# Prompt attention of a hybrid decoder step: query blocks in pairs, value parts side by side as the stationary operand, a feature-major result

## The chip, the core and the metric

The kernel runs on one core of one Trainium2 chip. The metric is device time in microseconds (us) of one execution. Five engines with queues of their own take part: TensorE (PE, which multiplies and transposes), VectorE (DVE), ScalarE (ACT), GpSimd (POOL) and SyncE (SP, which here only issues transfers). Each engine takes the instructions of its queue in order, and an instruction that waits holds up all that stand behind it on its engine.

## What is computed

The program is one step of a two-layer decoder, for a prompt of 1024 tokens and for a sample group of 64 tokens. The part in question is the attention of layer 0 over the prompt: 8 heads, 96 query and key features (64 and 32 rotated ones), 64 value features, causal:

```python
s = (jnp.einsum('bqhd,bkhd->bhqk', qn, k_nope)
     + jnp.einsum('bqhr,bkr->bhqk', qr, k_rope)).astype(jnp.float32) * SOFTMAX_SCALE
s = jnp.where(mask[None, None], s, -jnp.inf)
p = jax.nn.softmax(s, axis=-1)
lat = jnp.einsum('bhqk,bkc->bqhc', p.astype(c.dtype), c)
return jnp.einsum('bqhc,chv->bqhv', lat, w_uv).reshape(b, tq, ATTN_OUT_DIM)
```

The kernel forms the values (latent rows times `w_uv`) first and multiplies the probabilities with them. The 512 attention features stand beside 512 features of a pooling mixer, and the 1024 together are the operand of one output projection.

## The kernel before

Everything is float32. Where two float32 operands meet on PE, a factor is split in two float32r parts (a cast, and a subtraction of the cast from the whole) whose products are added up; this is how scores and projections are done.

`prompt_attention` (from L696) goes through the heads one by one, and in a head through eight blocks i of 128 queries, in the order 7, 0, 6, 1, 5, 2, 4, 3, so that a long block alternates with a short one. Of each block:

- **Scores** (`scores`, L730 to L756): three matmuls of split parts for each chunk of keys, plus a bf16 matmul that lays the mask on the diagonal (L744), into a tile `s` of two PSUM banks, of which there are two. On DVE follow the row maximum `mx` (L750) and its product with the scale `nmx` (L751), on ACT the exponential `p` with the row sum (L753), on DVE the reciprocal `ri` of the sum (L754). P isn't normalised here.
- **Transposes** (`transposes`): PE turns each 128x128 block of P into the tile `ptp` (L764), up to four in one PSUM bank of which there are three (shared with the transposes of queries and keys, `qkt`), and one copy for each bank brings them to SBUF as `pT`: on ACT the banks that begin at key block 0 of i from 2 up (L769), on DVE the others (L767).
- **Values** (`values`, L777): for each key block one float32 matmul with `pT` as the stationary operand and 64 columns of `v_sb` moving. A float32 matmul is two passes on PE. The result has queries on the partitions, and DVE multiplies it by `ri` on its way out (L780).

The steps of different blocks overlap: block n's scores are written out ahead of block n-1's transposes and of block n-2's values, and between the blocks PE also makes the next head's transposed queries and keys (`prep`: transposes L720, a cast on ACT and a subtraction on DVE, L722 and L723). From this text a scheduler sets each engine's order. For each pair of heads SP stores the result token-major to `a_d` in DRAM (L804).

The sample group's attention comes next, and while it ends, the operands of the output projection are loaded (`mix_load`, L1120 on): the mixer's 512 features feature-major from `mix_d`, by chunk of tokens in two loads of two row groups each, cast on ACT and subtracted on DVE and POOL (L1127 to L1130), and the attention's token-major rows from `a_d` in loads of one or two token blocks, which PE transposes (`mix_tokens`, `atp`, L1147), four blocks for each 128 tokens, before the same split (L1150, L1151). All these loads go through three buffers `raw`.

Of the kernel before, what the change touches and what calls it, by code (L numbers as in the profile page):

```python
# [10 lines left out]
F32 = mybir.dt.float32  # L11
# [4 lines left out]
ALU = mybir.AluOpType  # L16
# [52 lines left out]
def bank(g, kind, name):  # L69
    """One PSUM bank of [128, 512], from the banks that serve this kind of use in turn."""  # L70
# [16 lines left out]
def wunit(g, ap, a, b, ring, lo=None):  # L87
    """One [128, a, b] block of a weight, split into two float32r parts that add up to it."""
# [41 lines left out]
def mm3(g, ps, pairs):  # L130
    """Accumulate float32 products of split operands: ((wh, wl), (xh, xl)) per row block."""
# [8 lines left out]
# ------------------------------------------------------------------ constants  # L140
# [19 lines left out]
def bcast_cols(g, ps, dg, r, out, n):  # L160
    """out[:, t * 128 + q] = r[q, t] on every partition: columns of per-token numbers as one row."""
# [7 lines left out]
# ------------------------------------------------------------------ feature-major norm  # L169
# The next product runs on x * gain; the row of 1 / rms, one number per token, multiplies its result.  # L170
# [37 lines left out]
def later(g, *fn):  # L208
    """Put off what the tensor engine would wait for."""
    g.late += fn  # L210
# [8 lines left out]
# ------------------------------------------------------------------ MLP  # L219
# [46 lines left out]
class OutProj:  # L266
    """y += w.T @ X per chunk, then the operands and the scale of the next product."""
# [46 lines left out]
def in_even(g, I, O, S, st_left):  # L314
# [3 lines left out]
    with ExitStack() as st:  # L318
# [90 lines left out]
        def zproc(ci, tb0, nb, zs, sq):  # L409
# [34 lines left out]
            # latent and rotary key  # L444
# [88 lines left out]
def pool_mixer(g, I, O, S, X, rs0, w, ps, ut, keep):  # L533
# [46 lines left out]
        # trailing window sums by doubling, the last group in two pieces  # L580
# [65 lines left out]
# ------------------------------------------------------------------ layer 0: keys and values  # L646
# [49 lines left out]
def prompt_attention(g, I, S, v_sb, first, mix0):  # L696
    nc = g.nc
    with ExitStack() as st:
# [8 lines left out]
        heads = {}  # L707
        ao = {}
# [911 lines left out]
```

## Time and profile before

| what | value |
|---|---|
| median of 3 runs | 2839.73 us (2837.73 to 2841.03) |
| span of the profiled execution | 2838.5 us |
| PE busy | 2713.7 us (96%) |
| DVE busy | 1807.2 us (64%) |
| ACT busy | 898.8 us (32%) |
| POOL busy | 396.8 us (14%) |
| prompt attention | about 234 to 421 us of the span |
| loads and splits for the output projection | about 785 to 822 us |

The span runs from the first to the last instruction of one profiled execution; the runs' median lies 1.2 us above it. Busy shares are over the whole span, most of which is the two MLPs and the recurrent layer; what the change touches are the two stretches in the last rows.

### The profile page before, as it was taken

Reading aid. Unit: us, or ns where it says so; the run is one execution under the profiler, and the core shown is the slowest. Engines: PE = TensorE matmul, PEld = TensorE weight load, DVE = VectorE, ACT = ScalarE, POOL = GpSimd, SP = SyncE. Lnnn points to the kernel's source line nnn. Section 1 sums busy time; section 2 is a strip of 40 time slices with the busy share of each in tenths; the row PEclk is TensorE's granted clock in tenths of the full one; section 3 lists DMA queues with packets and bytes.
Section 4 is the critical chain, followed back from the end, with each engine's and each line's share of the span. In section 5 each row is a group of like instructions: output and inputs, shape, how many; then the busy total and the mean of one; then the engine's idle time right before and its main releaser. Section 6 shows DMA issues by size and latency. Waiting matters only on the chain.

```text
span 2838.5 us, 43000 instructions
## 1 busy us (share of the span) xinstructions
PE 2713.7 (96%) x16801; PEld 2632.6 (93%) x16801; DVE 1807.2 (64%) x3501; ACT 898.8 (32%) x1878; POOL 396.8 (14%) x453
## 2 busy tenths in 40 slices
PE   7998999999999999999999998987999999999999
PEld 6887989888899999999999988887999999999998
DVE  7665657888755555555555579998365555555555
ACT  5334555666634111111111146655321111111111
POOL 4321001232212000000000044555200000000000
PEclk9999998999999999999999999998999999999999
DMA  5233102222251111111111121113111111111111
GB/s 161 62 108 108 38 16 76 62 61 59 70 136 42 45 45 46 42 49 39 49 40 48 36 90 35 35 31 109 47 47 50 39 48 39 49 38 51 38 38 64
DMA packets 200743, 162.07 MB, mean 57 GB/s; under 512 B 40331, under 2 KB 183148, under 8 KB 199763
## 3 DMA queue, kind: packets, MB, share of 16 engines
q1 hardware_dynamic: 200539, 159.31, 18.9%
q8 instruction: 133, 2.18, 0.3%
q14 instruction: 71, 0.58, 0.1%
HBM read 138.18 MB, written 21.21 MB: 56 GB/s over the span
## 4 chain that ended last, share of the span: by engine, by line
PE 62%; DVE 8%; ACT 1%; DMA 1%; POOL 1%; issue 1%; ACTq 0%; DVEq 0%; POOLq 0%
PE up L136 26%; PE dn L136 26%; PE op L136 6%; PE pgt L136 2%; DVE hs L1372 1%; DVE xl L182 1%; PE pg L136 1%; PE pu L136 1%; DVE v L1339 1%; DVE ta L1362 1%; DVE q L1392 0%; DVE y L250 0%; DVE vl L80 0%; ACT whA L79 0%; PE nbc L165 0%
## 5 line engine op out<-in xcount | busy, mean ns | idle before, releaser
L250 DVE TENSOR_TENSOR y<-y,dn 128x384 f32<-128x384 f32 (+1 forms) x768 | 404.9, 531 | 282.0 <-PE dn L136 279.7
L136 PE MATMUL dn<-hh,whB 128*128 128x384 f32 (+1 forms) x1536 | 505.8, 329 | 3.9 <-DVE y L250 3.8
L136 PE MATMUL up<-xh,wlA 128*128 128x384 f32 (+1 forms) x1536 | 501.6, 327 | 0.0
L136 PE MATMUL up<-xh,whA 128*128 128x384 f32 (+1 forms) x1536 | 501.1, 326 | 0.0
L136 PE MATMUL dn<-hh,wlB 128*128 128x384 f32 (+1 forms) x1536 | 501.0, 326 | 0.0
L136 PE MATMUL up<-xl,whA 128*128 128x384 f32 (+1 forms) x1536 | 501.0, 326 | 0.0
L136 PE MATMUL dn<-hl,whB 128*128 128x384 f32 (+1 forms) x1536 | 500.7, 326 | 0.0
L79 ACT CAST whB<-raw 128x1024 fp32r<-128x1024 f32 (+3 forms) x80 | 79.9, 1034 | 703.5 <-PE dn L136 663.4
L136 PEld LDWEIGHTS dn<-hh,whB 128*128 128x128 f32 x1536 | 288.3, 188 | 11.8 <-DVE y L250 11.6
L136 PEld LDWEIGHTS up<-xh,wlA 128*128 128x128 f32 x1536 | 288.3, 188 | 0.4
L136 PEld LDWEIGHTS up<-xh,whA 128*128 128x128 f32 x1536 | 288.3, 188 | 0.3
L136 PEld LDWEIGHTS dn<-hl,whB 128*128 128x128 f32 x1536 | 288.4, 188 | 0.1
L136 PEld LDWEIGHTS up<-xl,whA 128*128 128x128 f32 x1536 | 288.3, 188 | 0.2
L136 PEld LDWEIGHTS dn<-hh,wlB 128*128 128x128 f32 x1536 | 288.3, 188 | 0.0
L235 DVE SCALAR_TENSOR_TENSOR rl<-up,rs 128x384 f32<-128x384 f32 (+1 forms) x192 | 102.8, 535 | 260.3 <-PE up L136 260.3
L236 ACT ACTIVATE hh<-rl 128x384 fp32r<-128x384 f32 (+1 forms) x192 | 97.1, 506 | 447.7 <-DVE rl L235 447.7
L80 POOL TENSOR_TENSOR wlA<-raw,whA 128x1024 fp32r<-128x1024 f32 (+2 forms) x24 | 58.4, 2435 | 769.2 <-ACT whA L79 766.7
L136 PE MATMUL pk<-wqh,cl 128*128 128x256 f32 (+1 forms) x512 | 153.3, 305 | 12.7 <-DVE cl L925 12.6
L136 PE MATMUL pk<-wqh,ch 128*128 128x320 f32 (+1 forms) x512 | 160.1, 315 | 0.7 <-ACT ch L924 0.7
L79 ACT CAST whA<-raw 128x1024 fp32r<-128x1024 f32 (+2 forms) x94 | 98.0, 1042 | 184.8 <-PE up L136 143.2
L237 DVE TENSOR_TENSOR rl<-rl 128x384 f32<-128x384 f32 (+1 forms) x192 | 106.0, 552 | 77.5 <-ACT hh L236 77.5
L136 PE MATMUL pk<-wql,ch 128*128 128x256 f32 (+1 forms) x512 | 151.9, 298 | 1.2 <-DVE wql L80 1.2
(558 smaller groups left out, 5378.5 us busy)
## 6 DMA issues: line engine op xcount, KB each, us to landing
raw<-in_w_up_dram SPq DMA_DIRECT2D x64, 512.0 KB
raw<-in_w_down_dram SPq DMA_DIRECT2D x64, 512.0 KB
cp<-in_cache_ckv_dram SPq DMA_DIRECT2D x128, 128.0 KB
raw<-in_w_in_rnn_dram SPq DMA_DIRECT2D x16, 512.0 KB
xt<-in_x_prompt_dram SPq DMA_DIRECT2D x8, 512.0 KB
raw<-in_w_out_even_dram SPq DMA_DIRECT2D x8, 512.0 KB
raw<-in_x_prompt_dram SPq DMA_DIRECT2D x8, 512.0 KB
raw<-in_w_out_rnn_dram SPq DMA_DIRECT2D x8, 512.0 KB
```

The source lines that it names most:

```text
L79: g.nc.scalar.copy(h, src)
L80: (lo or g.nc.vector).tensor_tensor(l, src, h.bitcast(F32), ALU.subtract)
L136: g.nc.tensor.matmul(ps, a, b, start=(i == 0), stop=(i == n - 1))
L182: nc.vector.scalar_tensor_tensor(xl[:, m], yv, gcol[:, m:m + 1], xh[:, m].bitcast(F32), ALU.mult, ALU.subtract)
L235: nc.vector.scalar_tensor_tensor(r[:, :n], ps[:, :n], 0.0, RS[c][:, :n], ALU.max, ALU.mult)
L236: nc.scalar.activation(hh[:, a:b], r[:, :n], AF.Square)
L237: nc.vector.tensor_tensor(r[:, :n], r[:, :n], r[:, :n], ALU.mult)
L250: nc.vector.tensor_tensor(y[c][:, m], y[c][:, m], ps[:, :n], ALU.add)
L1339: V.scalar_tensor_tensor(v, ul[:, a + k:b + k], vec[:, k, n:n + 1], v, ALU.mult, ALU.add)
L1362: V.scalar_tensor_tensor(ta[:, a:b], a0[:, a:b], 1.0, ta[:, a:b], ALU.add, ALU.mult)
L1372: V.tensor_tensor_scan(hs[:, a:b], a0[:, a:b], ig[:, a:b], hs[:, a - 1:a] if a else 0.0, ALU.mult, ALU.add)
```

## The change

The queries go through in pairs of blocks (2ip and 2ip+1), ip in the order 3, 0, 2, 1, so blocks in the order 7, 6, 1, 0, 5, 4, 3, 2. In a pair:

- P is normalised at once: GpSimd multiplies `p` by `ri` in place. Blocks above 3 have two buffers `p`, the others two buffers `p4` (three `p` for all before).
- The transposes are grouped by pairs of key blocks: one bank holds up to four blocks (two key blocks of two query blocks; three where the diagonal cuts one off). Each bank is split: ACT casts it to `pTh`, DVE subtracts to `pTl`.
- The values of a head are split in two parts that lie side by side in `vt` (a cast on ACT, a subtraction on POOL, once a head). `vt` of a key block, 128x128, is the stationary operand, and 256 columns of `pTh` and then of `pTl` move (128 columns for the key block that only the second query block sees). The result has features on the partitions: the high part's product in rows 0 to 63, the low part's in rows 64 to 127.
- ACT copies that result to `ao` by pairs (L803). After a head's last pair, SP stores rows 0 to 63 to `mix_d`, which now has 1024 rows (L806), and a DMA issued by POOL adds rows 64 to 127 to them in DRAM (L807).
- `mix_load` takes all 1024 features feature-major: four loads for each chunk of tokens, cast and subtracted as before, and only the sample tokens are still transposed. `a_d` is gone.

The rest of the diff takes out comments.

```diff
 def prep(h, part):
     if part == 0:
+        vt = vts[h] = at.tile([P, 8, 2, VH], F32R, name="vt", tag="vt")
+        split(g, vt[:, :, 0], vt[:, :, 1], v_sb[:, :, h], nc.gpsimd)
...
-            p_ = at.tile([P, SEQ], F32, name="p", tag="p", bufs=3)
+            p_ = at.tile([P, SEQ if i > 3 else 512], F32, name="p", tag="p" if i > 3 else "p4")
             nc.scalar.activation(p_[:, :nk], sv, AF.Exp, bias=nm, scale=SCALE, accum_out=sm)
             nc.vector.reciprocal(ri, sm)
-            P_[(h, i)] = (p_, ri)
+            nc.gpsimd.tensor_scalar_mul(p_[:, :nk], p_[:, :nk], ri)
+            P_[(h, i)] = p_
...
-                pT = at.tile([P, 512], F32, name="pT", tag="pT", bufs=6)
-                if j0 or i < 2:
-                    nc.vector.tensor_copy(pT[:, :nj * P], pt[:, :nj * P])
-                else:
-                    nc.scalar.copy(pT[:, :nj * P], pt[:, :nj * P])
+                th = at.tile([P, 512], F32R, name="pTh", tag="pTh", bufs=6)
+                tl = at.tile([P, 512], F32R, name="pTl", tag="pTl", bufs=5)
+                nc.scalar.copy(th[:, :n], pt[:, :n])
+                nc.vector.tensor_tensor(tl[:, :n], pt[:, :n], th[:, :n].bitcast(F32), ALU.subtract)
...
-                nc.tensor.matmul(po[:, :VH], tiles[j // 4][:, (j % 4) * P:(j % 4 + 1) * P], v_sb[:, j, h], start=(j == 0), stop=(j == i))
-            nc.vector.tensor_scalar_mul(ao[h // 2][:, i, (h % 2) * VH:(h % 2 + 1) * VH], po[:, :VH], ri)
+                    for x, t in enumerate(parts):
+                        nc.tensor.matmul(out, vts[h][:, j].rearrange("p s d -> p (s d)"), t[:, cs],
+                                         start=(j == 0 and x == 0), stop=(lone and x == 1))
+            nc.scalar.copy(ao[h][:, ip * 2 * P:(ip + 1) * 2 * P], PO.pop((h, ip))[:, :2 * P])
+            if ip == 1:
+                rows = S.mix_d[512 + h * VH:512 + (h + 1) * VH, :SEQ]
+                nc.sync.dma_start(rows, ao[h][:VH])
+                nc.gpsimd.dma_start(rows, ao[h][VH:], accum_op=ALU.add)
...
-        seq = [(h, i) for h in range(H) for i in (7, 0, 6, 1, 5, 2, 4, 3)]
+        seq = [(h, ip) for h in range(H) for ip in (3, 0, 2, 1)]
...
 def mix_load(g, S, X, c):
-    for gi in (0, 2):
+    for gi in (0, 2, 4, 6):
+        e = n if gi < 4 else min(b, SEQ) - a
...
-    for tb in range(3 * c, min(3 * c + 3, 8), 2):
-        nb = 2 if tb + 1 < min(3 * c + 3, 8) else 1
-        at = raw_tile(g)[:, :1024].rearrange("p (a b) -> p a b", a=2)
-        nc.sync.dma_start(at[:, :nb], S.a_d[tb * P:(tb + nb) * P, :].rearrange("(a p) d -> p a d", p=P))
-        for j in range(nb):
-            mix_tokens(g, X, tb + j, at[:, j])
```

How the engines' orders move is shown at three places of a head in the middle of the stage. PE between the scores of block 6 and those of the block that takes over block 6's tile `s` (block 5 before, block 0 after). The kernel before, from behind block 6's mask on (its L741 rows are block 1's scores, and at the end the first of block 5's; `po` x8 are block 7's values):

```order
L720 MATMUL qkt<-ident,qh 96x128 x4
L764 MATMUL ptp<-ident,p 128x128
L777 MATMUL po<-v_sb,pT 128x64 x8
L741 MATMUL s<-kth,qth 128x256
L741 MATMUL s<-ktl,qth 128x256
L741 MATMUL s<-kth,qtl 128x256
L744 LDWEIGHTS idb
L744 MATMUL s<-mneg,idb 128x128
L720 MATMUL qkt<-ident,qh 96x128 x4
L777 MATMUL po<-v_sb,pT 128x64
L764 MATMUL ptp<-ident,p 128x128 x7
L741 MATMUL s<-kth,qth 128x384
```

The changed kernel, from the mask of block 1 on (block 6 stands ahead of block 1, with four `po` of the head before between them; `vt` is the value parts' tile, and the last row is the first of block 0's scores):

```order
L747 MATMUL s<-mneg,idb 128x128
L723 MATMUL qkt<-ident,qh 96x128 x4
L797 MATMUL po<-pTh,vt 128x256
L797 MATMUL po<-pTl,vt 128x256
L797 MATMUL po<-pTh,vt 128x256
L797 MATMUL po<-pTl,vt 128x256
L797 MATMUL po<-pTh,vt 128x256
L797 MATMUL po<-pTl,vt 128x256
L797 MATMUL po<-pTh,vt 128x128
L797 MATMUL po<-pTl,vt 128x128
L744 MATMUL s<-kth,qth 128x256
```

Values in one-pass matmuls of 256 columns have taken the place of two-pass ones, and the block that reuses block 6's tile now stands one block nearer to it.

ACT around the exponential of block 5 (128x768). Before:

```order
L722 CAST qth<-qkt 96x512
L753 ACTIVATE p,sm<-s,nmx 128x896
L722 CAST qth<-qkt 96x512
L753 ACTIVATE p,sm<-s,nmx 128x256
L769 COPY pT<-ptp 128x512
L722 CAST kth<-qkt 96x512
L753 ACTIVATE p,sm<-s,nmx 128x768
L722 CAST kth<-qkt 96x512
```

The changed kernel; `pTh` are the casts of transposed probabilities, `ao` the copy of a pair's result:

```order
L756 ACTIVATE p,sm<-s,nmx 128x128
L774 CAST pTh<-ptp 128x512 x2
L725 CAST qth<-qkt 96x512
L774 CAST pTh<-ptp 128x512
L774 CAST pTh<-ptp 128x384
L725 CAST kth<-qkt 96x512
L774 CAST pTh<-ptp 128x384
L725 CAST kth<-qkt 96x512
L756 ACTIVATE p,sm<-s,nmx 128x768
L803 COPY ao<-po 128x256
L756 ACTIVATE p,sm<-s,nmx 128x640
```

Between the exponential of the last block of a pair ahead (128x128, block 0) and that of block 5 now stand five casts of `pTh`, one of queries and two of keys; before, one copy and one cast stood between the exponentials of blocks 1 and 5.

POOL through a part of a head. Before, POOL has nothing to do in the heads; what stands around the stage is the mask's constant, two weight splits, and then the sample attention's first operands:

```order
L704 MEMSET mneg 128x128
L705 AFFINE_SELECT mneg<-mneg 128x128
L80 TENSOR_TENSOR wlA<-raw,whA 128x1024 x2
L877 COPY q_4922<-q_s 64x1024
L879 MEMSET qbd 128x2048
L898 MEMSET msk 64x64
```

The changed kernel, in a head in the middle:

```order
L758 TENSOR_SCALAR p<-p,ri 128x1024
L758 TENSOR_SCALAR p<-p,ri 128x896
L758 TENSOR_SCALAR p<-p,ri 128x256
L80 TENSOR_TENSOR vt<-v_sb,vt 128x8x64
L758 TENSOR_SCALAR p<-p,ri 128x128
L807 DMA mix_d<-ao 64x1024
L758 TENSOR_SCALAR p<-p,ri 128x768
L758 TENSOR_SCALAR p<-p,ri 128x640
```

Each block's P now passes through POOL, and the accumulating DMA of the head before, which waits for SP's store of the same rows, stands between the passes of block 0 and block 5.

## Rows read from the trace of the kernel before

**Rows 1.** Windows: busy us and (count) of PE, PEld, DVE, ACT, POOL; clock.

```profile
340.00:380.00 40.00, 39.62 (x317) 36.20 (x317) 27.35 (x83) 22.56 (x50) 0.00 (x0) 1.00 0.01 1
421.00:443.00 22.00, 20.12 (x105) 17.74 (x104) 11.17 (x20) 7.37 (x18) 4.18 (x7) 0.50 0.32 88
500.00:540.00 40.00, 36.70 (x265) 34.34 (x266) 32.29 (x60) 24.91 (x79) 11.45 (x18) 1.00 0.22 57
```

**Rows 2.** Timeline of PE: start, us, instruction; two heads' first scores, then values and scores.

```profile
310.14 0.48 PE L741 MATMUL s<-kth,qth 96*128 96x512 f32 x1
...
331.54 0.48 PE L741 MATMUL s<-kth,qth 96*128 96x512 f32 x1
...
344.48 0.38 PE L764 MATMUL ptp<-ident,p 128*128 128x128 f32 x2
344.70 1.67 PE L777 MATMUL po<-v_sb,pT 128*128 128x64 f32 x14
346.19 0.42 PE L741 MATMUL s<-kth,qth 96*128 96x384 f32 x1
...
348.32 0.36 PE L741 MATMUL s<-kth,qth 96*128 96x256 f32 x1
348.52 0.28 PE L741 MATMUL s<-ktl,qth 96*128 96x256 f32 x1
348.64 0.28 PE L741 MATMUL s<-kth,qtl 96*128 96x256 f32 x1
```

**Rows 3.** Groups by form, 260 to 380 us: count, busy, mean ns, idle before.

```profile
L769 ACT COPY pT<-ptp 128x512 f32<-128x512 f32 x28 | 16.3, 582 | 16.2 <-PE ptp L764 16.2
L780 DVE TENSOR_SCALAR ao<-po,ri 128x64 f32<-128x64 f32 x46 | 12.9, 281 | 13.1 <-PE po L777 13.1
...
L723 DVE TENSOR_TENSOR ktl<-qkt,kth 96x512 fp32r<-96x512 f32 x12 | 8.2, 682 | 1.8 <-ACT kth L722 1.8
...
L754 DVE RECIPROCAL ri<-sm 128x1 f32<-128x1 f32 x46 | 7.1, 155 | 6.5 <-ACT p L753 5.7
...
L751 DVE TENSOR_SCALAR nmx<-mx 128x1 f32<-128x1 f32 x45 | 6.6, 148 | 0.4
...
L750 DVE TENSOR_REDUCE mx<-s 128x1 f32<-128x896 f32 x5 | 5.5, 1091 | 3.1 <-PE s L744 3.1
...
L753 ACT ACTIVATE p<-s,nmx 128x896 f32<-128x896 f32 x5 | 5.0, 1007 | 4.4 <-DVE nmx L751 4.4
L750 DVE TENSOR_REDUCE mx<-s 128x1 f32<-128x640 f32 x6 | 4.9, 824 | 1.0 <-PE s L744 0.9
...
L753 ACT ACTIVATE p<-s,nmx 128x640 f32<-128x640 f32 x6 | 4.8, 794 | 1.8 <-DVE nmx L751 1.8
```

**Rows 4.** Groups by form on POOL, whole span.

```profile
L80 POOL TENSOR_TENSOR wlA<-raw,whA 128x1024 fp32r<-128x1024 f32 x20 | 49.9, 2493 | 766.0 <-ACT whA L79 763.4 <-PE pg L136 2.6
...
L80 POOL TENSOR_TENSOR wpl<-raw,wph 128x512 fp32r<-128x512 f32 x1 | 1.3, 1289 | 1.6 <-ACT wph L79 1.6
...
L877 POOL COPY q<-q_s 64x1024 f32<-64x1024 f32 x1 | 1.0, 1034 | 125.5 <-PE qkt L720 125.5
```

**Rows 5.** Waits from 234 to 262 us: total, times, longest.

```profile
PE ptp L764 <- ACT p L753: 9.5, 2, 5.8
...
ACT whA L79 <- DMA raw<-in_w_out_even_dram: 6.1, 1, 6.1
```

**Rows 6.** Timeline of PE at the end of the stage.

```profile
416.51 1.30 PE L777 MATMUL po<-v_sb,pT 128*128 128x64 f32 x10 [0.50 <-ACT pT L769]
...
418.93 1.53 PE L777 MATMUL po<-v_sb,pT 128*128 128x64 f32 x8 [0.68 <-ACT pT L769]
```

**Rows 7.** Waits of PE in the sample attention, 460 to 760 us.

```profile
PE pk L136 <- DVE cl L925: 12.6, 11, 2.5
```

**Rows 8.** Output projection's operands, 785 to 822 us: the transposes on PE.

```profile
L1147 PE MATMUL atp<-ident,raw x36: 222/272/299, 792.2 to 812.5; 128*128 128x128 f32 x32, 64*128 64x64 f32 x4
```

**Rows 9.** The same stretch: a wait of POOL.

```profile
POOL xl L1130 <- ACT xh L1128: 11.3, 4, 5.2
```

More of the change, by code (lines that the diff above doesn't have):

```diff
@@ L773, in values @@
-        def values(h, i):
-            tiles, ri = PT.pop((h, i))
-            po = ps.tile([P, 512], F32, name="po", tag="po", bufs=1)
-            for j in range(i + 1):
-                nc.tensor.matmul(po[:, :VH], tiles[j // 4][:, (j % 4) * P:(j % 4 + 1) * P], v_sb[:, j, h], start=(j == 0), stop=(j == i))
-            if h % 2 == 0 and h // 2 not in ao:
-                ao[h // 2] = at.tile([P, 8, 2 * VH], F32, name="ao", tag="ao", bufs=2)
-            nc.vector.tensor_scalar_mul(ao[h // 2][:, i, (h % 2) * VH:(h % 2 + 1) * VH], po[:, :VH], ri)
+            nc.gpsimd.tensor_scalar_mul(p_[:, :nk], p_[:, :nk], ri)
@@ new lines, in prompt_attention, with values @@
+        PO = {}
+        def values(h, ip, banks):
+            for b in banks:
+                if b > ip:
+                    continue
+                if b == 0:
+                    PO[h, ip] = ps.tile([P, 512], F32, name="po", tag="po", bufs=1)
+                po = PO[h, ip]
+                parts = PT.pop((h, ip, b))
+                for jj in range(2):
+                    j = 2 * b + jj
+                    lone = j == 2 * ip + 1
+                    out = po[:, P:2 * P] if lone else po[:, :2 * P]
+                    cs = slice(2 * P, 3 * P) if lone else slice(jj * 2 * P, (jj + 1) * 2 * P)
+                    for x, t in enumerate(parts):
+                        nc.tensor.matmul(out, vts[h][:, j].rearrange("p s d -> p (s d)"), t[:, cs],
+                                         start=(j == 0 and x == 0), stop=(lone and x == 1))
+            if ip not in banks:
+                return
+            if h not in ao:
+                ao[h] = at.tile([P, SEQ], F32, name="ao", tag="ao", bufs=2)
+            nc.scalar.copy(ao[h][:, ip * 2 * P:(ip + 1) * 2 * P], PO.pop((h, ip))[:, :2 * P])
[3 more added lines that the diff above has]
+                nc.gpsimd.dma_start(rows, ao[h][VH:], accum_op=ALU.add)
@@ L784, in prompt_attention @@
         mix0(lambda: ps.tile([P, 512], F32, name="pm_", tag="pt", bufs=3))
-        seq = [(h, i) for h in range(H) for i in (7, 0, 6, 1, 5, 2, 4, 3)]
-        for n, (h, i) in enumerate(seq):
-            scores(h, i)
-            if n % 8 in (2, 3, 4, 5) and h + 1 < H:
-                prep(h + 1, n % 8 - 2)
-            if n >= 1:
-                transposes(*seq[n - 1])
-            if n >= 2:
-                values(*seq[n - 2])
-                ph, pi = seq[n - 2]
-                if ph % 2 and n % 8 == 1:
-                    store(nc, S, ao, ph // 2)
-        transposes(*seq[-1])
-        values(*seq[-2])
-        values(*seq[-1])
-        store(nc, S, ao, 3)
-def store(nc, S, ao, hp):
-    nc.sync.dma_start(S.a_d[:SEQ, hp * P:(hp + 1) * P].rearrange("(b p) d -> p b d", p=P), ao[hp])
+        seq = [(h, ip) for h in range(H) for ip in (3, 0, 2, 1)]
+        for n, (h, ip) in enumerate(seq):
+            old, older = (seq[n - k] if n >= k else None for k in (1, 2))
+            for half in range(2):
+                scores(h, 2 * ip + 1 - half)
+                if h + 1 < H and n % 4 in (1, 2):
+                    prep(h + 1, 2 * (n % 4 - 1) + half)
+                if older:
+                    values(*older, (0, 1) if half == 0 else (2, 3))
+                if old:
+                    transposes(*old, (0, 1) if half == 0 else (2, 3))
+        values(*seq[-2], (0, 1, 2, 3))
+        transposes(*seq[-1], (0, 1, 2, 3))
+        values(*seq[-1], (0, 1, 2, 3))
 def sample_attention(g, I, S, ahead, fill_start, fill):
@@ L1426, in step @@
     S.k_d = dr.tile([SEQ, H * QH], F32, name="k_d")
-    S.mix_d = dr.tile([512, T], F32, name="mix_d")
-    S.a_d = dr.tile([T, 512], F32, name="a_d")
+    S.mix_d = dr.tile([1024, T], F32, name="mix_d")
     S.y_d = [dr.tile([P, KB, b - a], F32, name=f"y_d{c}") for c, (a, b) in enumerate(CH)]
```

30 lines of the change are left out of this document (17 added, 13 removed).

## The prediction

> **What bounds the kernel now.** I read the windows of the attention stage first. In the middle of it PE is busy for 39.62 of 40 us at full clock, DVE for 27.35, ACT for 22.56 and POOL not at all [rows 1]. So PE sets the pace, and only the stage's ends have waits worth naming. The timeline gives the head's length: block 7's scores start at 310.14 and again at 331.54, 21.40 us a head [rows 2], 21.2 of them PE's. The groups by form then give each operation's price [rows 3].
>
> **PE's work in a head.** A head has 36 key blocks of values, each a float32 matmul of two passes. Fourteen passes stand between 344.70 and 346.19, 0.106 each [rows 2], so 72 take 7.7 us. Now there are 32 one-pass matmuls of 256 columns and 8 of 128. Split score matmuls of 256 columns follow each other 0.12 apart (348.52, 348.64); those of 128 columns I put at the 0.11 of a transpose (344.48 to 344.70, two of them) [rows 2]. That is 3.84 + 0.88 = 4.7 us: PE's work falls by 3.0 us, to 18.2 a head. The number of transposes stays.
>
> **The other engines' sums.** Ten banks a head, 4608 columns, are now both cast on ACT and subtracted on DVE, where one copy did before. At 0.582 and 0.682 for 512 columns [rows 3] that is 5.2 us on ACT and 6.1 on DVE. ACT loses its copies (2944 columns, 3.3 us) and gains four copies of 256 columns (some 0.4 each, by columns from the 0.582) and the cast of the values, 0.58; from 12.1 us a head (22.56 of 40 times 21.40) it goes to 16.1. DVE loses copies of 1664 columns (some 2.2) and eight outputs of 0.281, and goes from 14.6 to 16.3. POOL gets 4608 columns of scaling, the values' subtraction (1.289 for 512 columns [rows 4]) and a DMA issue: 7 to 13 us by the price below. None reaches 18.2. By sums alone PE would stay the bound and gain 24 us.
>
> **The scaling on POOL** is the unknown price; the trace has none. From below stands POOL's copy, one input and one output, 1.034 for 1024 columns; from above its operation on two tiles, 2.49 [rows 4]. A cost below nothing is excluded, since the step is new and on the way. It reads one tile and one number for each row, so the copy is nearer: I take 1.1 for 1024 columns, and keep 2.4 for the range. On this the Trainium skill, GPSIMD Engine Reference, section 4.1 Engine selection, speaks against the change: elementwise work belongs on VectorE, GpSimd being about half as fast with two inputs, though near line rate with one. Read as a ban it gives the upper row's price and 2852 us (the second rival); its clause on one input gives the copy's, and the sum below; that the two rows differ by 2.4 backs the clause.
>
> **Why the queues give most of it back.** Before, a long block alternated with a short one, and the values' 7.7 us lay as cover between scores and whatever waited for their softmax. Now blocks run 7, 6, 1, 0, 5, 4, 3, 2, the cover is 3 us shorter, and P takes one stop more. I followed one head in the middle through the four queues by the changed order, each instruction starting at the later of its engine's turn and its input, with prices from rows 3 and some 0.1 to 0.2 for a hand-over. Three waits of PE come out.
>
> First, block 0's scores need the tile that block 6's exponential frees. From block 6's mask PE has four values (0.46), block 1's scores (three of 0.12, 0.08 on the first and the mask, 0.5), four transposes of queries (0.43) and eight values (0.93): 2.3 us. Meanwhile ACT's next instruction is the query cast, whose transposes end at 1.4; it runs to 2.1, the exponential of 896 columns (1.007) to 3.1, and with the hand-over PE goes on at 3.3: a wait of 1.0. The maximum (1.091) and `nmx` (0.148) are done by then [rows 3].
>
> Second, block 3's scores need block 5's exponential, which stands on ACT behind the second key cast. From that cast's transposes PE has 0.9 us of values; the cast (0.49), the exponential of 768 columns (0.90, between the rows of 640 and 896) and hand-overs take 1.75: a wait of 0.85.
>
> Third, eleven transposes need block 4's scaled P. From block 4's mask PE has key transposes (0.43), values (0.93), the wait just named, block 3 (0.87), values (0.46) and block 2 (0.7): 4.2 us. DVE first ends block 5's work and reaches block 4's maximum at 0.9 (0.824), and the scale `nmx` behind a key subtraction (0.682) at 2.4; the exponential of 640 columns (0.794) ends at 3.4, the reciprocal (0.155) stands behind block 3's maximum and comes at 4.1, POOL's 640 columns (0.7) end near 5.0: a wait of 1.0.
>
> Some 0.2 more goes to transposes that wait for a bank, since each is held by two readings in turn. So a head takes 18.2 + 1.0 + 0.85 + 1.0 + 0.2 = 21.2 us, against 21.40. Seven heads of steady running give -1.4.
>
> **The stage's ends.** At the start ACT waits 6.1 us for a weight load, and block 6's exponential stands behind that; PE's transposes wait up to 5.8 for it [rows 5]. In the changed order the exponentials of 896, 256 and 128 columns and two casts stand ahead of the weight, so they are done when it lands. At least the two longer exponentials are won, 1.5 us, at most all of PE's 5.8; I take -3.5, the three exponentials and two casts. At the end PE waits 0.50 and 0.68 for copies [rows 6]; now the last pair has POOL's pass (0.5) and a subtraction (0.6) more in its chain, about +1. The last accumulating DMA stands on POOL ahead of the sample attention's first copy (1.034, done long before till now [rows 4]) and of a memory fill; PE has 20 us of other work in 421 to 443 [rows 1], so I cost it at nothing; uncovered it would be 3 to 5 us.
>
> **POOL's DMA in each head** waits for SP's store to land, and the scaling of block 5 is queued behind it, then blocks 4 to 2. From block 0's exponential to block 5's, ACT has eight casts and PE the scores of blocks 5 and 4: about 8 us of cover. The landing isn't shown; a load landed within the 6.1 us that ACT waited [rows 5]. I take nothing.
>
> **The output projection's operands.** Of 36 transposes 32 go, 3.5 us of PE at 0.11 [rows 8]. POOL gets six more subtractions of up to 1.4 us where it waits 11.3 for ACT [rows 9]. Loads through three buffers become twelve where there were eleven. Between 0 and -4; I take -2.6.
>
> **The sum.** -1.4 - 3.5 + 1 - 2.6 = -6.5 on the profiled span of 2838.5, which lies 1.2 below the median: **2833 us**. A measurement here tells about 0.2%, 5.7 us, from no change, so this is just past that line, with perhaps 8 us of error in the waits (1 us a head).
>
> **Rivals.**
>
> - *The waits stay hidden.* PE keeps working ahead, a head takes 18.2 to 18.5: -24 - 2.6, about 2813. For it speaks that no engine's sum reaches 18.2; against it that engines take their queues in order and `s` has two tiles. 0.12.
> - *POOL's pass is dear (the slower side).* At 2.4 for 1024 columns the eight transposes of the first pair wait 1.3 us longer for blocks 7 and 6, one behind the other on POOL (2.4 + 2.1), the eleven 0.7, the seven 0.4: 2.4 us a head, 19 in all, 2852. By proportion from 1.1 it cancels the whole gain at 1.5 and is measurably slower from 1.9. Traffic of DVE beside it could stretch it too. 0.14. The same page of the Trainium skill (section 3.1, Elementwise, side-by-side cycle accounting) gives 1.8 cycles an element at 1.2 GHz as the best of a tight loop; an estimate from that is 1.5 us for 1024 columns and so 2840 us; no run so far shows it, and the copy's row stands below it.
> - *The clock falls.* PE is at 1.20 GHz (0.50) through 421 to 443, after the waits of 0.50 and 0.68 and thin work there [rows 1, 6]. If each head's three waits did the same for 2 to 5 us, it would cost 1 to 2.5 us a head: 2841 to 2853. Against it: in the sample attention PE waits 11 times, up to 2.5 us [rows 7], and between 500 and 540 us it is busy for only 36.70 of 40 at full clock [rows 1]. 0.07.
> - *Values don't run at 0.12.* If 256 columns with 128 rows contracted took two passes' time, PE's work would be 22 a head instead of 18.2, part of it inside the waits: about 2845. Score rows of the same type speak against it. 0.04.
>
> **How the numbers follow.** The forecast has 0.63. Of it 0.35 lies below 2834, and the rest, 0.28, within 0.2% of no change. With the first rival faster has 0.47, same 0.28, and the three slower rivals 0.25. The range leaves out about 0.1 on each side: from 2816, which cuts through the first rival, to 2852, the dear pass.
>
> **What would show it.** Right: a head of about 21.2 us between block 7's scores; PE waits before block 0's and block 3's scores with ACT's exponential as releaser, and before the eleven transposes with POOL as releaser, each near 1 us; values 0.12 apart; scaling of 1024 columns near 1.1; PE's clock full in the heads. Wrong: heads of 18 to 19 us without such waits, scaling above 1.5, a clock below full in mid-stage, PE waiting for block 5's P because POOL stood at its DMA, or the operands' stretch no shorter.

## The result and the profile after

The changed kernel takes **2882.41 us** (median of 4 runs, 2880.16 to 2884.04) against 2838.73 us of the kernel before (4 runs): 1.0154 times as long, with a 95% interval of 1.0140 to 1.0168. The forecast was 2833 us with 2816 to 2852 as its range; the kernel became slower by 44 us instead of faster by 6.

Where the time went is read from five places that both programs have, each the first PE instruction of its kind in the profiled executions, and from the span's end (us from the span's start):

| place | before | after | difference | added since the place above |
|---|---|---|---|---|
| first scores of the prompt attention | 234.8 | 242.4 | +7.6 | +7.6 |
| first transposes behind it (`qst`) | 420.4 | 471.5 | +51.1 | +43.5 |
| first products of the sample attention (`pk`) | 437.3 | 483.5 | +46.2 | -4.9 |
| first transposes of the residual (`xtp`, L1174 before) | 764.0 | 808.9 | +44.9 | -1.3 |
| second weight group of the output projection (`op` with `whB`) | 822.6 | 864.4 | +41.8 | -3.1 |
| end of the span | 2838.5 | 2880.6 | +42.1 | +0.3 |

So the loss is in the heads, with a smaller one ahead of them, and some is given back behind. The windows (columns as in [rows 1]) show mid-stage:

```profile
300.00:340.00 40.00, 30.91 (x196) 27.00 (x196) 21.84 (x53) 21.57 (x50) 23.00 (x15) 0.88 0.24 60
```

PE is busy for 30.91 of 40 us where it was for 39.62 [rows 1], and its clock is 0.88 of full. DVE, ACT and POOL are busy for 22 to 23 of 40: no engine is a bound, so the time lies in waits. PE's, from 262 to 430 us (total, times, longest):

```profile
PE ptp L770 <- POOL p L758: 27.6, 14, 2.4
PE s L744 <- ACT p L756: 8.0, 11, 0.8
```

In the timeline of PE one head from block 7's scores (297.49) to the next (325.73) takes 28.2 us; over five heads it is 28.1, against 21.40 [rows 2]. The bracket at a row's end is the idle time ahead of it and who ended it:

```profile
297.49 0.60 PE L744 MATMUL s<-kth,qth 96*128 96x512 f32 x1
...
306.88 0.39 PE L744 MATMUL s<-kth,qth 96*128 96x256 f32 x1 [0.78 <-ACT p L756]
...
310.59 1.30 PE L770 MATMUL ptp<-ident,p 128*128 128x128 f32 x8 [2.26 <-POOL p L758]
...
319.67 0.50 PE L744 MATMUL s<-kth,qth 96*128 96x512 f32 x1 [0.67 <-ACT p L756]
...
324.19 1.89 PE L770 MATMUL ptp<-ident,p 128*128 128x128 f32 x11 [2.35 <-POOL p L758]
325.73 0.78 PE L744 MATMUL s<-kth,qth 96*128 96x512 f32 x1
326.30 0.63 PE L744 MATMUL s<-ktl,qth 96*128 96x512 f32 x1
326.73 0.63 PE L744 MATMUL s<-kth,qtl 96*128 96x512 f32 x1
...
328.79 0.28 PE L797 MATMUL po<-pTh,vt 128*128 128x256 f32 x1
328.91 0.28 PE L797 MATMUL po<-pTl,vt 128*128 128x256 f32 x1
...
330.51 0.40 PE L744 MATMUL s<-ktl,qth 96*128 96x512 f32 x1
330.74 0.39 PE L744 MATMUL s<-kth,qtl 96*128 96x512 f32 x1
```

Four waits come to 6.1 us a head: 0.78 and 0.67 for the exponential ahead of blocks 0 and 3, and 2.26 and 2.35 for POOL's scaled P ahead of eight and eleven transposes. Behind a wait for POOL the clock falls to 1.20 GHz: the 512-column matmuls of 326.30 and 326.73 stand 0.43 apart, those of 330.51 and 330.74 again 0.23. The values stand 0.12 apart (328.79, 328.91), as forecast. POOL's scaling, by form (count, busy, mean ns):

```profile
L758 POOL TENSOR_SCALAR p<-p,ri 128x1024 f32<-128x1024 f32 x8 | 22.8, 2848 | 38.4 <-DVE ri L757 38.4
...
L758 POOL TENSOR_SCALAR p<-p,ri 128x640 f32<-128x640 f32 x8 | 15.0, 1873 | 0.0
...
L758 POOL TENSOR_SCALAR p<-p,ri 128x128 f32<-128x128 f32 x8 | 4.8, 601 | 0.0
```

The pass over 1024 columns takes 2.85 us: 0.28 us and 2.51 ns for each column. Both rows that were to bound it, 1.03 and 2.49 [rows 4], lie below. On POOL's timeline three such passes stand one behind the other (1024, 896 and 256 columns, 6.25 us), and the accumulating DMA takes 0.83 us of POOL and holds nobody up, since the next block's P comes 6 us later:

```profile
333.10 6.25 POOL L758 TENSOR_SCALAR p<-p,ri 128x1024 f32<-128x1024 f32 x3 [4.74 <-DVE ri L757]
...
340.57 0.60 POOL L758 TENSOR_SCALAR p<-p,ri 128x128 f32<-128x128 f32 x1
341.12 0.83 POOL L807 DMA_DIRECT2D mix_d<-ao  x1
348.08 2.19 POOL L758 TENSOR_SCALAR p<-p,ri 128x768 f32<-128x768 f32 x1 [6.13 <-DVE nmx L754]
```

The later start stands on ACT. The cast of the first head's values waits for the stores of `so` (output rows on their way from SBUF to DRAM), and the first query casts are queued behind it:

```profile
236.90 0.62 ACT L79 CAST vt<-v_sb 128x512 fp32r<-128x512 f32 x1 [4.82 <-DMA out_dram<-so]
```

### The profile page after: what moved, and what is told of

It is laid out like the page before. It is cut to its first block, busy times and chain, and to the rows that moved or that the text cites. A ratio compares the mean times of both kernels' runs of the same rounds, so it can differ in the third digit from the quotient of the medians.

```text
span 2880.6 us, 42656 instructions
## 1 busy us (share of the span) xinstructions
PE 2706.9 (94%) x16513; PEld 2617.9 (91%) x16513; DVE 1821.2 (63%) x3467; ACT 927.5 (32%) x1948; POOL 528.8 (18%) x539
## 3 DMA queue, kind: packets, MB, share of 16 engines
q1 hardware_dynamic: 197547, 159.31, 18.6%
## 4 chain that ended last, share of the span: by engine, by line
PE 61%; DVE 8%; ACT 1%; POOL 1%; issue 1%; DMA 1%; ACTq 0%; DVEq 0%; POOLq 0%
PE up L136 26%; PE dn L136 26%; PE op L136 5%; PE pgt L136 2%; DVE hs L1388 1%; DVE xl L182 1%; PE pu L136 1%; PE pg L136 1%; DVE v L1355 1%; DVE ta L1378 1%; DVE q L1408 0%; DMA raw<-mix_d 0%; DVE y L250 0%; DVE vl L80 0%; PE otp L1566 0%
```

## The experiments

Each kernel is a small edit of the changed one. The scheduler sets the order anew for each, so a few other instructions move with every edit. "Head" is the mean distance of block 7's first scores over four to six heads in mid-stage. The ratios of the experiments are to runs of the kernel before on each experiment's own chip (15 to 21 runs with medians of 2837.3 to 2837.8 us), so they aren't the quotients of this table's medians; e13_const has one run.

| kernel | median us (runs) | ratio to before, 95% | head us | first scores | first `qst` |
|---|---|---|---|---|---|
| before | 2838.73 (4) | | 21.4 | 234.8 | 420.4 |
| changed | 2882.41 (4) | 1.0154 (1.0140 to 1.0168) | 28.1 | 242.4 | 471.5 |
| e1_dve | 2834.61 (10) | 0.9995 (0.9985 to 1.0005) | 22.0 | 242.9 | 425.6 |
| e2_none | 2822.50 (4) | 0.9949 (0.9932 to 0.9967) | 20.1 | 242.9 | 410.5 |
| e3_vt_late | 2878.96 (2) | 1.0146 (1.0119 to 1.0174) | 28.2 | 237.6 | 470.5 |
| e4_warm | 2872.34 (2) | 1.0123 (1.0099 to 1.0147) | 26.0 | 242.3 | 459.3 |
| e10_part | 2834.96 (8) | 0.9989 (0.9979 to 0.9999) | 21.7 | 243.8 | 425.3 |
| e13_const | 2858.63 (1) | | 24.4 | 243.0 | 449.3 |
| e6_dve_vt | 2827.70 (5) | 0.9965 (0.9951 to 0.9980) | 21.0 | 236.2 | 419.9 |
| e7_dve_vtdve | 2829.56 (5) | 0.9965 (0.9951 to 0.9980) | 21.0 | 235.0 | 417.3 |
| e5_split_vt | 2838.48 (10) | 1.0002 (0.9992 to 1.0013) | 22.4 | 238.9 | 431.2 |
| e9_act67 | 2837.37 (10) | 1.0004 (0.9994 to 1.0014) | 22.2 | 236.7 | 424.4 |
| e11_prep23 | 2824.32 (4) | 0.9950 (0.9933 to 0.9967) | 20.7 | 237.3 | 417.1 |
| e12_prep13 | 2836.98 (10) | 1.0000 (0.9990 to 1.0010) | 23.0 | 234.6 | 425.4 |

### Is it POOL's pass? Scaling on DVE, no scaling, and scaling at the forecast's price

```diff
-            nc.gpsimd.tensor_scalar_mul(p_[:, :nk], p_[:, :nk], ri)
+            nc.vector.tensor_scalar_mul(p_[:, :nk], p_[:, :nk], ri)
```

> The changed kernel with the scaling of P on DVE instead of POOL. Theory 1 (the scaling's price on POOL, 2.85 us for 1024 columns, sets PE's waits before the eight and the eleven transposes): on DVE the pass takes 0.6 to 1.2 us for 1024 columns, both waits fall from 2.3 us to under 1, the clock stays full inside the heads, a head takes 20.5 to 22 us instead of 28 and the time is 2820 to 2840 us. Rival A (what costs is the order of blocks and the two score tiles, whatever engine scales): a head stays above 25 us and the time above 2855 us. Rival B (DVE becomes the bound: its 16 us a head and the added passes): DVE busy above 95 per cent in mid-stage, a head of 21.5 to 23 us, 2835 to 2850 us.

The head falls from 28.1 to 22.0 us and the clock is 1.00 from 260 to 380 us. DVE takes 0.75 us for 1024 columns, as these groups from 260 to 400 us show:

```profile
L758 DVE TENSOR_SCALAR p<-p,ri 128x256 f32<-128x256 f32 x6 | 8.3, 1378 | 0.0
...
L758 DVE TENSOR_SCALAR p<-p,ri 128x1024 f32<-128x1024 f32 x6 | 4.5, 746 | 0.0
...
L758 DVE TENSOR_SCALAR p<-p,ri 128x384 f32<-128x384 f32 x6 | 2.5, 410 | 0.0
```

PE no longer waits for a scaled P; what it waits for, from 262 to 400 us, is above all the exponential that frees a score tile:

```profile
PE s L744 <- ACT p L756: 11.7, 13, 1.1
PE po L797 <- ACT pTh L774: 2.9, 6, 0.5
```

Theory 1 holds and rival A falls: neither the order of the blocks nor the two score tiles make the 28 us. DVE is busy for 36.97 of 40 us (300 to 340 us), 92 per cent and not rival B's 95, but the head lies in rival B's range and the time 0.4 us below it: a bound by DVE isn't ruled out.

```diff
-            nc.gpsimd.tensor_scalar_mul(p_[:, :nk], p_[:, :nk], ri)
```

> The changed kernel without the scaling of P: the normalisation is left out and everything else stays, so the time shows what the rest of the change does with the step at no cost. Theory 1: waits for the scaling gone, clock full in mid-stage, a head of 20 to 20.6 us, time 2815 to 2825 us, with the later start of the stage (6 us) still in it. Rival A (order and score tiles): a head above 24 us, time above 2850 us.

With no scaling a head takes 20.1 us, and PE's waits in one (timeline, 283 to 304 us) are these three, 1.6 us:

```profile
290.35 0.38 PE L796 MATMUL po<-pTl,vt 128*128 128x256 f32 x1 [0.75 <-DVE pTl L774]
...
292.01 1.10 PE L769 MATMUL ptp<-ident,p 128*128 128x128 f32 x8 [0.62 <-ACT p L756]
...
301.09 0.55 PE L769 MATMUL ptp<-ident,p 128*128 128x128 f32 x3 [0.21 <-ACT p L756]
```

This is what the change gives with the step at no price: 1.3 us a head, not the 3.0 that was taken off PE's work. PE is busy for 18.6 us of this head, where 21.2 were before and 18.2 were forecast.

```diff
-            nc.gpsimd.tensor_scalar_mul(p_[:, :nk], p_[:, :nk], ri)
+            nc.gpsimd.tensor_scalar_mul(p_[:, :nk * 5 // 16], p_[:, :nk * 5 // 16], ri)
```

> The changed kernel with POOL scaling only the first 5/16 of each block's columns (320 of 1024); the rest of the normalisation is left out. By the measured 0.28 us plus 2.51 ns a column, the pass of a 1024-column block then takes 1.08 us, the price that the prediction took. If only that price was wrong: a head of 20.8 to 21.6 us as forecast (21.2), full clock in the heads, and a time of 2829 to 2838 us, since the later start of the stage (6 us) is still in it. Rival (the bookkeeping of the queues was wrong too): a head above 22.5 us or below 20.3 us.

A block of 1024 columns now has a pass of 1.08 us, the price that the forecast took. The time, 2834.96 us, lies in the foreseen range; the head is 21.7 us in the mean, a little above the range's edge of 21.6, and the clock 0.98 (290 to 370 us). Group and waits (262 to 400 us):

```profile
L758 POOL TENSOR_SCALAR p<-p,ri 128x320 f32<-128x320 f32 x8 | 8.7, 1083 | 16.8 <-DVE ri L757 16.1 <-PE ptp L770 0.7
```

```profile
PE ptp L770 <- POOL p L758: 6.1, 13, 0.7
PE s L744 <- ACT p L756: 5.3, 12, 0.6
```

So the price, with the clock that falls behind it, makes 6.4 of the 6.7 us that a head lost. That the mean comes within 0.5 us of the forecast is partly luck, for two kinds of heads stand in it (windows of two heads, one behind the other):

```profile
309.73:330.47 20.74, 18.90 (x139) 16.45 (x138) 15.60 (x39) 14.75 (x36) 8.30 (x11) 1.00 0.16 26
330.47:353.78 23.31, 20.34 (x140) 17.65 (x138) 15.53 (x39) 15.01 (x36) 7.67 (x10) 0.93 0.12 24
```

Of six heads three take 20.7 us and one 21.7, at full clock, and two take 23.3 with the clock at 0.93. In the first of the two shown PE's waits before block 0, before block 3 and before the eleven transposes are 0.51, 0.43 and 0.57 us, about half of what was forecast, and PE's work is 18.9 us instead of 18.2. In the second PE waits before the seven and the eight transposes, before values and before block 0, never longer than 0.74 us, and yet the clock falls.

### Why is the pass dear? A constant in place of the row's number

```diff
-            nc.gpsimd.tensor_scalar_mul(p_[:, :nk], p_[:, :nk], ri)
+            nc.gpsimd.tensor_scalar_mul(p_[:, :nk], p_[:, :nk], 0.5)
```

> The changed kernel with P multiplied on POOL by the number 0.5 instead of each row's reciprocal: the normalisation is left out, the pass and its place stay. It asks why the pass (2.85 us for 1024 columns) lies outside both rows that bounded it, the copy (1.03) and the operation on two tiles (2.49). Theory: the number read for each row is what costs, and with a constant the pass falls to the copy's 1.0 to 1.3 us, the head to 21 to 22 us, the time to 2830 to 2842 us. Rival: any arithmetic of this form on POOL takes 2.5 ns a column, the pass stays at 2.7 to 2.9 us, and the time at 2875 to 2885 us.

```profile
L758 POOL TENSOR_SCALAR p<-p 128x1024 f32<-128x1024 f32 x8 | 22.2, 2772 | 30.4 <-ACT p L756 30.4
```

The pass stays at 2.77 us, as the rival said: the number read for each row isn't the cause (0.08 us of it), and the theory falls. Yet the head is 24.4 us instead of 28.1, and the time of the one run, 2858.63 us, lies in neither range. Here P's pass waits for neither the row sum's read nor the reciprocal and starts that much earlier (its releaser is now ACT's exponential); PE's waits for POOL shrink with it, to a longest of 1.8 us (262 to 420 us), and the clock is 0.91 (300 to 380 us):

```profile
PE ptp L770 <- POOL p L758: 19.0, 13, 1.8
```

In a head PE waits 3.66 us in all (0.78, 1.25 and 1.63) instead of 6.06; the other 1.3 us of the gain go with the clock, which was not tested apart here. The copy that served as the lower bound has 64 partitions; one with 128 partitions in the kernel before is cheap too, 0.43 us for 256 columns where the scaling of 256 takes 0.92, so the partitions aren't the cause either:

```profile
L680 POOL COPY kk<-kr 128x256 f32<-128x256 f32 x8 | 3.4, 427 | 22.2 <-DVE rsu L119 10.5 <-DMA k_d<-kk 8.8 <-DVE kr L311 2.0
```

Why this form takes 2.5 ns a column stays open; a pass that isn't in place wasn't tried.

### The clock's share: PE kept at work while it waits

```diff
                 pt = ps.tile([P, 512], F32, name="ptp", tag="pt", bufs=3)
+                if b == 0 and ip > 1:
+                    for _ in range(18):
+                        nc.tensor.transpose(pt[:, :P], g.ident, g.ident)
```

> The changed kernel with 18 transposes of the identity (1.9 us at full clock) ahead of the first transposes of the pairs with six and eight key blocks, into the same PSUM bank, overwritten by the real ones: PE works where it waited for POOL. Theory 2 (the clock that falls behind the two waits of 2.3 us costs some 3 us a head beyond the waits themselves): the clock stays at 1.00 in mid-stage, a head takes 24.5 to 25.5 us instead of 28.2, time 2855 to 2863 us. Rival: the added work only delays, or the clock's fall is hidden inside the next wait for POOL: a head stays at 28 us, time 2880 us or more.

The clock is 1.00 (300 to 380 us) and the head 26.0 us (PE's waits for POOL from 262 to 430 us):

```profile
300.00:380.00 80.00, 70.14 (x530) 61.06 (x530) 46.66 (x116) 47.40 (x109) 49.15 (x32) 1.00 0.19 40
```

```profile
PE ptp L773 <- POOL p L758: 16.6, 19, 1.7
```

The direction is theory 2's, its size too large: the low clock costs 2.1 us a head net, not 3, since much of what PE does faster only ends in a longer wait for POOL: the fill of 1.9 us and the wait of 1.7 that is left before the eight transposes come to 3.6, where the wait alone was 2.26. The total falls by 10 us (12 by the first `qst`) instead of 19 to 27.

### The later start

```diff
             if part == 0:
-                vt = vts[h] = at.tile([P, 8, 2, VH], F32R, name="vt", tag="vt")
-                split(g, vt[:, :, 0], vt[:, :, 1], v_sb[:, :, h], nc.gpsimd)
...
             nc.vector.tensor_tensor(tl[:QH, cs], pt[:QH], th[:QH, cs].bitcast(F32), ALU.subtract)
+            if part == 3:
+                vt = vts[h] = at.tile([P, 8, 2, VH], F32R, name="vt", tag="vt")
+                split(g, vt[:, :, 0], vt[:, :, 1], v_sb[:, :, h], nc.gpsimd)
```

> The changed kernel with each head's split of the values written behind the last query and key split of its preparation instead of ahead of them, so that in memory and on ACT the values' parts no longer stand where 8 output rows are still being stored. Theory: the 4.8 us that ACT waits at 232 us for those stores go, the first scores start at 236 to 237 instead of 242.4 us, time 5 to 6 us less, 2876 to 2877 us. Rival: the first scores wait for something else that is ready no earlier (weights, the mixer's result), and the time stays at 2881 to 2883 us.

The first scores start at 237.6 instead of 242.4, as foreseen, but the stage ends only 1.0 us earlier (470.5 against 471.5): the first head alone, 30.1 us instead of 27.2, takes 2.9 of the 4.8 back. The two runs (2875.65 and 2882.27) don't settle the total.

The same edit on top of scaling on DVE:

> Scaling on DVE, and the split of the values written behind the query and key splits. Theory: the stage starts 5 us earlier than with the scaling on DVE alone and the heads stay at 22.0 us, so the time is 3 to 5 us below that kernel, 2829 to 2832 us. Rival: the earlier start is lost again in the first head, which waits for a weight load, and the time stays within 2 us of that kernel.

The time is 1.3 us below the expected range and below both the kernel before and e1_dve, but by another way. Of the 6.7 us that the first scores come earlier, 1.0 is left at the second head (265.64 against 266.62): ACT waits for the weight load that [rows 5] already showed, and PE behind it (timelines of ACT and PE):

```profile
254.67 1.04 ACT L79 CAST whA<-raw 128x1024 fp32r<-128x1024 f32 x1 [5.60 <-DMA raw<-in_w_out_even_dram]
```

```profile
257.08 0.87 PE L771 MATMUL ptp<-ident,p 128*128 128x128 f32 x3 [4.53 <-DVE pTl L776]
```

The rival was right on this. The gain comes from heads of 21.0 us instead of 22.0. What differs in them is a pair of rows of e1_dve, DVE's 256-column pass and POOL's subtraction of the values (timelines of DVE and POOL):

```profile
320.24 1.38 DVE L758 TENSOR_SCALAR p<-p,ri 128x256 f32<-128x256 f32 x1
```

```profile
320.20 1.27 POOL L80 TENSOR_TENSOR vt<-v_sb,vt 128x512 fp32r<-128x512 f32 x1 [17.50 <-ACT vt L79]
```

DVE's pass began at 320.24, 0.04 us behind POOL's instruction, and ended 0.15 us behind it, and so in all six heads looked at. In e6_dve_vt POOL's subtraction begins 0.23 us behind the start of that pass, which then takes 0.345 us instead of 1.378; the next pass, of 128 columns, begins while POOL is still at it, takes 0.37 instead of 0.286 and ends 0.09 us behind POOL:

```profile
L759 DVE TENSOR_SCALAR p<-p,ri 128x256 f32<-128x256 f32 x6 | 2.1, 345 | 0.0
L759 DVE TENSOR_SCALAR p<-p,ri 128x128 f32<-128x128 f32 x6 | 2.2, 370 | 0.2
```

PE's two waits behind the long pass in e1_dve (0.48 us for ACT's `pTh`, 0.16 for DVE's `pTl`) are gone with it.

With that subtraction on DVE altogether (e6's kernel with `split(g, ..., v_sb[:, :, h], nc.vector)`):

> As the kernel with scaling on DVE and the later split of the values, with that split's subtraction on DVE instead of POOL. In the run with scaling on DVE the 256-column pass took 1.38 us where 384 columns take 0.41, and it ended with POOL's subtraction beside it. Theory (DVE's pass from SBUF to SBUF waits while POOL works on SBUF): the outlier goes, every pass keeps to about 0.15 us plus 0.58 ns a column, DVE gains 1.0 and loses 0.6 us a head, a head takes 21.4 to 22.0 us. Rival (the form of 256 columns is slow by itself, or waits for something else): it stays at 1.3 us and the head gets 0.3 to 0.6 us longer.

The 256-column pass takes 0.347 us, but it nearly did in e6_dve_vt; the 128-column pass is back at 0.286, and the head is 20.97 us in both. The theory's mechanism holds, its gain had been taken.

### What is left of PE's waits

In e6_dve_vt PE waits twice a head, both times for the exponential that frees a score tile (1.10 us ahead of block 0's scores, 0.67 ahead of block 3's; in all, from 262 to 400 us):

```profile
PE s L745 <- ACT p L757: 10.7, 12, 1.1
```

Four kernels asked what sets these.

Short blocks scaled on POOL (on top of the later split):

```diff
-            nc.gpsimd.tensor_scalar_mul(p_[:, :nk], p_[:, :nk], ri)
+            (nc.vector if i > 3 else nc.gpsimd).tensor_scalar_mul(p_[:, :nk], p_[:, :nk], ri)
```

> Blocks 4 to 7 scaled on DVE, blocks 0 to 3 (128 to 512 columns, 0.6 to 1.56 us) on POOL, and the later split of the values. Theory: DVE, busy for 92 per cent with all of the scaling, sheds about 2.5 us a head and POOL's short passes fit into the cover of the seven and three transposes: a head of 20.5 to 21.5 us, 2820 to 2828 us. Rival A: DVE's passes wait for POOL's more often and the head stays at 22 us or more, 2829 to 2836 us. Rival B: blocks 3 and 2 (1.56 and 1.25 us, one behind the other) make PE wait before the seven transposes, head above 22 us with POOL as releaser.

The theory falls: the head is 22.4 us. PE's waits (the first is the last one of a head, the others are of the next):

```profile
311.46 0.45 PE L745 MATMUL s<-kth,qth 96*128 96x384 f32 x1 [1.22 <-ACT p L757]
...
316.38 0.98 PE L771 MATMUL ptp<-ident,p 128*128 128x128 f32 x7 [0.24 <-POOL p L759]
...
322.28 0.39 PE L745 MATMUL s<-kth,qth 96*128 96x256 f32 x1 [1.34 <-ACT p L757]
```

Rival B isn't it (0.24 us for POOL); nor is rival A, since DVE's passes keep their prices (0.745 us for 1024 columns). The waits for score tiles grew to 1.2 to 1.3 us in an order that had changed throughout; what in that order does it stays open. They are only part of the miss: with the same three waits some heads take 21.6 us at full clock and others 23.15 with the clock at 0.93.

Blocks 7 and 6 scaled on ACT (`nc.scalar.activation(p_[:, :nk], p_[:, :nk], AF.Copy, scale=ri)`), the others on DVE, on top of e7_dve_vtdve (waits from 262 to 400 us):

> Scaling of blocks 7 and 6 on ACT, of the others on DVE; the values' split late, its subtraction on DVE. ACT has some 14.6 us of work a head and DVE 19.4; this moves 1.4 us off DVE and puts 2.1 on ACT. Theory (PE's waits are for ACT's exponentials in ACT's order, not for DVE's load): ACT's longer queue makes them longer, head 21.3 to 22.5 us, 2830 to 2840 us. Rival (DVE's load is what counts): head 20 to 20.6 us, 2820 to 2826 us.

```profile
PE s L745 <- ACT p L757: 17.3, 24, 1.8
```

DVE has less to do (112.6 of 135 us busy from 265 us on, where e7_dve_vtdve has 125.1) and the head is longer, 22.2 us: 24 waits for ACT's exponential instead of 13. ACT's queue counts here, not DVE's load.

Query and key preparation one pair later:

```diff
-                if h + 1 < H and n % 4 in (1, 2):
-                    prep(h + 1, 2 * (n % 4 - 1) + half)
+                if h + 1 < H and n % 4 in (2, 3):
+                    prep(h + 1, 2 * (n % 4 - 2) + half)
```

> Scaling on DVE and the later split of the values (head 20.97 us, 2827.7 us), with the next head's query and key preparation written one pair later, so that no query or key cast stands on ACT ahead of the exponentials of blocks 6 and 5. Theory: PE's two remaining waits a head (1.1 us before block 0's scores, 0.7 before block 3's, both for ACT's exponential) come from those casts and shrink; head 19.5 to 20.5 us, 2817 to 2825 us. Rival: DVE, 92 per cent busy, is what ends the chain (its maximum and nmx come late), and the head stays at 20.8 to 21.5 us with the waits elsewhere, 2826 to 2833 us.

2824.32 us is below the kernel before and in the expected range, though the head, 20.7 us, is outside it; against e6_dve_vt the gain isn't settled, since the intervals overlap. In mid-stage the heads alternate between 19.6 and 21.85 us, both at full clock; these are PE's waits around a long one (timeline, 303 to 324 us):

```profile
305.82 0.50 PE L745 MATMUL s<-kth,qth 96*128 96x512 f32 x1 [0.55 <-ACT p L757]
...
314.09 0.38 PE L745 MATMUL s<-kth,qth 96*128 96x256 f32 x1 [1.06 <-ACT p L757]
...
316.65 0.44 PE L745 MATMUL s<-kth,qth 96*128 96x384 f32 x1 [0.32 <-ACT p L757]
```

Block 0's wait (1.06) outlived the removal of the query cast, so that cast was not its only cause. With the queries where they were and only the keys later (`n % 4 in (1, 3)`):

> The same, with the queries' preparation where it was and the keys' one two pairs later: only the key casts leave block 5's exponential. Theory: block 3's wait (0.7 us) goes and block 0's (1.1 us) stays: head 20.3 us, 2822 to 2826 us. Rival: DVE sets the head's length, 20.8 us or more.

A head takes 23.0 us, and PE waits up to 0.8 us before the eight transposes and before the eleven, for DVE both times. The theory's gain isn't there and the rival's range holds, but the run doesn't test the keys' place alone. In five heads of six DVE's pass over 896 columns again begins just behind POOL's subtraction of the values and takes 1.72 us, where it takes 0.69 in the sixth (timelines of DVE and POOL):

```profile
317.27 1.73 DVE L759 TENSOR_SCALAR p<-p,ri 128x896 f32<-128x896 f32 x1
```

```profile
317.24 1.26 POOL L80 TENSOR_TENSOR vt<-v_sb,vt 128x512 fp32r<-128x512 f32 x1 [18.45 <-ACT vt L79]
```

And two of these heads, of 23.7 and 23.6 us, have the clock at 0.93; at full clock they take 22.3 to 22.9. In e11_prep23 the same collision stretches the 128-column pass of every other head to 0.85 us. The order of e11_prep23 with the subtraction on DVE was not run.

## Why the prediction was wrong

- **PE's work: right but for 0.4 to 0.7 us.** Values stand 0.12 apart, and nothing in the values themselves is slow. At full clock PE is busy for 18.6 us a head (e2_none) to 18.9 (e6_dve_vt, e10_part) instead of 18.2.
- **The price of scaling: the step that failed.** It was bounded by the copy (1.03) and the operation on two tiles (2.49), and the copy was taken because both read one tile. It measured 2.85 in place of the 1.1 taken, outside both ends, and put waits of 2.26 and 2.35 us before the eight and the eleven transposes; with the pass at 1.08 (e10_part) the head falls from 28.1 to 21.7. A bound from rows of other forms was treated as if arithmetic on one tile could not cost more than an operation on two. On the same point the Trainium skill (GPSIMD Engine Reference, section 4.1 Engine selection) says near line rate for one input; the trace differs, with 2.85 us for 1024 columns against DVE's 0.75, and the measurement decides. Its general rule, elementwise work on VectorE, is what e1_dve confirms.
- **The waits: mechanism right, one mis-sized by the price.** Foreseen were 1.0 ahead of block 0, 0.85 ahead of block 3 and 1.0 ahead of the eleven transposes; measured 0.78, 0.67 and 2.35. The fourth, 2.26 ahead of the eight, stood only in the rival of the dear pass. At the price taken (e10_part) the head is 21.7 against a forecast of 21.2, and the closeness is partly luck: more of PE's work and shorter waits in some heads, a lower clock in others.
- **The rivals: right one by one, wrong as alternatives.** The dear pass at 2.4 was given 2852 us, and by its own proportion 2.85 gives 2859. The falling clock was a case by itself with 0.07, at 1 to 2.5 us a head; in fact it comes with the dear pass and adds 2.1 us a head (e4_warm), 10 to 12 us of the time. Even at the price taken it falls in two heads of six (e10_part). Waits that come back in every head and a clock that may fall belong in one case.
- **The stage's start: a delay ahead of it left out.** The step took a gain of 3.5 us and looked only at the order around the weight load. It left out that the first head's value cast is a new first instruction on ACT, in memory where `so` was still being stored: 4.8 us of waiting, which e3_vt_late takes away. With that, two casts of 0.6 us, and a PE that was 1.2 us later already in the mixer's matmuls, the first scores come 7.6 us later. The first head then gets much of it back, 27.2 us instead of 32.6, so the second starts 2.3 us later (269.62 against 267.35), and at the price taken at the same time as before (267.31). Without the delay (e6_dve_vt) the first head is 8.5 us longer than the later ones, where it was 11.2 before, but it starts 1.4 us later too and ACT still waits for the weight load, so how much of the 3.5 the order gives isn't settled.
- **The stage's end: the sign right, a gain behind it not seen.** About +1 was taken. From the last head's first scores to `qst` it is 33.8 us, 5.7 more than a head, where before it was 3.2 more: +2.5. Behind the stage 4.9 us came back, of which the forecast has nothing: PE ran 421 to 443 us at 0.50 before [rows 1], where the changed kernel's same transposes run at full clock (`qst` 216 ns each instead of 311).
- **POOL's DMA: right.** Its issue takes 0.83 us, and block 5's P comes 6 us later.
- **The operands of the output projection: right.** -2.6 was taken; from `xtp` to the second weight group it is -3.1.

Together, in the profiled executions: +2.3 us to the second head (the forecast had -3.5), +39.8 in the six heads from there to the last (-1.2), +9.1 in the last head and the stage's end (-0.2 and +1), -4.9 behind it (nothing), -4.1 in the rest (-2.6). That is 42 us instead of -6.5. In e10_part, with the pass at the price taken, the six heads are 2.1 us longer than before instead of 39.8: almost all of that is the price and the clock that fell with it.

## What to carry to other kernels

A step that is moved to an engine that the trace doesn't show doing it has no upper bound from other forms: its price is the first thing to measure, or to place where its failing costs nothing. When waits are priced, price the clock with them, and when a new tile is added, ask which transfers are still under way in the memory that it gets and what stands behind its first writer. Here the paired layout pays once P is scaled on DVE and the values are split late (0.9965); whether the preparation one pair later (0.9950) gives more isn't settled.

## What the hardware showed

- POOL's multiplication of a tile by one number (a row's or a constant) takes 2.5 ns a column, in place, float32: 2.85 and 2.77 us for 128x1024, beside 1.03 for its copy of 64x1024 [rows 4] and 0.75 for DVE's same multiplication.
- DVE's multiplication from SBUF to SBUF, begun while POOL subtracted SBUF tiles, ended only behind POOL: 1.38 us instead of 0.345 for 256 columns (e1_dve), 1.72 instead of 0.69 for 896 (e12_prep13), 0.37 instead of 0.286 for 128 (e6_dve_vt). It ended 0.15, 0.50 and 0.09 us behind POOL's instruction, near what its columns cost: an estimate from DVE's 0.746 us for 1024 columns and 0.286 for 128 is 0.13, 0.46 and 0.07. POOL's subtraction kept to its 1.27 us. DVE's subtraction that reads PSUM kept to its 0.69 us inside POOL's (the changed kernel: DVE from 311.90 us, POOL from 311.40 to 312.67). The Trainium skill (GPSIMD Engine Reference, section 8 Key points) has the two engines sharing their SBUF interfaces, with contention for DVE instructions in a two-port mode or with two SBUF inputs; these rows agree that there is contention and put the whole wait on DVE, but none shows which mode DVE's pass was in.
- The granted clock went by more than the longest wait. With two waits of 2.3 us in a head of 28 us it was 0.88 in the mean, and full with PE kept busy in them (waits up to 1.7 us left). In the sample attention of the kernel before, single waits up to 2.5 us [rows 7] left it full [rows 1]. But heads of e10_part with no wait above 0.74 us had 0.93, and in e5_split_vt heads with the same waits (up to 1.35 us) had 0.93 or 1.00.
